# GLA on one core: ScalarE in written order, Exp and Ln from one table, a scratch in PSUM, token scales stored transposed, four weight casts on ScalarE

## The chip, the cores and the metric

One core of one Trainium2 chip. The metric is the device time of one execution in microseconds. The kernel before took 2317.13 us, the median of three runs (2316.85 to 2319.09).

## What is computed

One layer of a streaming encoder for 2048 prompt tokens and 32 sample tokens, model width 1024, all in float32. One projection feeds a windowed attention and a gated linear attention (GLA) side by side; their outputs are joined, projected and followed by a feed-forward part.

```python
n = rmsnorm(x);  z = n @ w_in                       # qa ka va | qg kg vg | rg | ca
log_a = log_sigmoid(ca @ w_alpha + b_alpha) / 16
# A: o = softmax(qa ka^T / 8, with a sink per head) va, over the own chunk of 64 and two before
# B, per chunk, with b = cumsum(log_a):
o_inter = (q * exp(b)) @ S
A = sum_k q[t] * exp(b[t] - b[s]) * k[s], s <= t;   o_intra = A @ v
S = exp(b_last) * S + (k * exp(b_last - b))^T @ v
gla = rmsnorm(o) * silu(rg)
h = x + concat(attn, gla) @ w_out
y = h + relu(rmsnorm(h) @ w_up)^2 @ w_down
```

## The kernel before

The prompt is cut into 16 tiles of 128 tokens; the sample is a seventeenth tile of 32. Every big product is made of three matmuls, since each operand is held as a rounded high part (`h`) and a remainder (`l`); `split_weight` (L194) loads a piece of a weight into a tile called `stage`, rounds it on ScalarE (L203) or VectorE (L205) and subtracts on GpSimd or VectorE (L207). `stage` and most other loads share five buffers, the io pool, so a load waits until a buffer comes free.

The work runs in three parts. In the **attention part** (0 to some 390 us) `front` (L253) loads a tile `xT1a` of transposed input, scales it and splits it into `nT`; `scales` computes the tile's rsqrt of the mean square into a column of `rstd`; `store` (L282) writes that column (`rs`) and the split tile (`nTh`, `nTl`) to DRAM, from where the GLA part reads them again. `project_q`, `project_kv` and `project_gate` make the projections, `attend` the softmax attention. Toward its end `prepare_gla` (L612) loads the GLA weights, each in two halves; `GLA_ENG` says for each half which engine rounds it and which subtracts.

In the **GLA part** (some 390 to 755 us) the tiles go in eight halves of two tiles (the first has the sample as a third). For each half `project` (L721) makes zq and zk, copied to `kq` with the token scales `rb` (rows of `rs` broadcast over the partitions, L631), and zv. `decay` (L641) makes the gates' logarithm for the next half: cc, then Abs, Exp and Ln on ScalarE, then a running sum (scan) on VectorE at L674; between Ln and the sum stands `gates` (L710), which loads `g` and applies Silu. `gla_tile` (L783) works on one tile: qkp, ec (Exp of the running sum), eight differences E on GpSimd, Abs and Exp of them on ScalarE in two groups of four, their products with k and q on VectorE (L823, L827); then the diagonal `dk` and its copy into `AT` (L839), the transposes of the last E into `dk` and their copy `kdT` (L854), the matmuls `A`, their masked copies into `AT` (L881 to L892), the output `go`, the state update `Sp` (L924), squares of the output `v<-go` (L930), `rsqrt` (L170, eleven small steps on VectorE), the gated output `g` (L936), its transposes and the copy `gT` (L945), stored to `mixT`. In the last half the first output weights `wo_00` to `wo_11` and mixed inputs `m0`, `m1` of the feed-forward part are loaded and split too (`prepare_ffn`, `load_mix`). The **feed-forward part** takes the rest.

TensorE's order is written by hand: every matmul depends on the one before it (`_pe`, L87), and generators that yield a number of nanoseconds are resumed by a clock (`tick`, L138). On ScalarE only the operations that need a function table are chained (`table`, L118); a table load is put in where the function asks for another one. Everything else on ScalarE, VectorE, GpSimd and in SP's queue of DMAs is ordered by a scheduler that simulates the engines.

Of the kernel before, what the change touches and what calls it, by code (L numbers as in the profile page):

```python
# [9 lines left out]
F32 = mybir.dt.float32  # L10
F32R = mybir.dt.float32r
I32 = mybir.dt.int32
AF = mybir.ActivationFunctionType
# [6 lines left out]
P = 128  # L20
# [7 lines left out]

class Builder:
    def __init__(self, ctx, tc, a, o, nt=NT, ffn=True):  # L30
# [3 lines left out]
        self.V, self.S, self.G, self.T, self.Q = nc.vector, nc.scalar, nc.gpsimd, nc.tensor, nc.sync  # L34
        pool = lambda name, bufs, **kw: ctx.enter_context(tc.tile_pool(name=name, bufs=bufs, **kw))
# [7 lines left out]
        tiles = list(range(nt)) + [nt]  # L43
# [5 lines left out]
        self.rsd = [dt([self.rows(t), 1], f"rs{t}") for t in tiles]  # L49
# [74 lines left out]

    def spawn(self, gen, delay=0):
        task = [self.clock + delay, self.seq, gen]
        self.seq += 1
        self.tasks.append(task)
        return task
# [40 lines left out]
    def rsqrt(self, ms, r, n, name, psum=False):  # L170

        V = self.V
        y = self.small.tile([P, 16], F32, tag="rsq_y", name=f"rsq_y_{name}")[:r, :n]
        if psum:
            q = self.ps_s(f"rsq_q_{name}")[:r, :n]
        else:
            q = self.small.tile([P, 16], F32, tag="rsq_q", name=f"rsq_q_{name}")[:r, :n]
# [53 lines left out]
    def attention_phase(self):  # L231
# [3 lines left out]
        with ExitStack() as ctx:  # L235
# [46 lines left out]
            def store(t):  # L282

                r = self.rows(t)
                Q.dma_start(self.rsd[t], self.rstd[:r, t : t + 1])
                if t == nt or t % 2:
                    for x, dst in zip(nT[t], self.nTd[t // 2]):
                        Q.dma_start(dst, x.bitcast(F32))

            order = [*range(10), nt, *range(10, nt)]  # L290
# [3 lines left out]
            V.memset(self.ones, 1.0)  # L294
            S.activation(self.rstd[:, :1], self.ones, AF.Square)
# [261 lines left out]
            for i, t in enumerate(order):  # L557
# [13 lines left out]
                if t == nt - 1:  # L571
                    self.prepare_gla(0)
# [21 lines left out]
    GLA_ENG = (("act", "pool"), ("dve", "dve"))  # L594
# [26 lines left out]
    def gla_tokens(self, h, tiles):  # L621
# [3 lines left out]
        off = 0  # L625
        for t in tiles:
# [4 lines left out]
            self.Q.dma_start(rb[:, off : off + r], self.rsd[t].rearrange("r o -> o r").broadcast_to([P, r]))  # L631
# [46 lines left out]
    def gla_phase(self):  # L678
        tc, a, V, S, G, Q = self.tc, self.a, self.V, self.S, self.G, self.Q
        nt = self.nt  # L680
        with ExitStack() as ctx:
# [28 lines left out]
            def gates(h):  # L710

                for t in halves[h]:
# [6 lines left out]
                    G.tensor_tensor(out=gv, in0=gv, in1=ggla[:r].unsqueeze(1).broadcast_to([r, 4, P]), op=ALU.mult)  # L719

# [62 lines left out]
            def gla_tile(n, t, off, kq, cc):  # L783
# [149 lines left out]
                rs = self.rsqrt(ss, L, 4, f"g{t}")  # L933
# [15 lines left out]
            gates(0)  # L949
            for h in range(len(halves)):  # L950
# [4 lines left out]
            self.finish()  # L955
            for key, name in (("p", "s_prompt"), ("s", "s_sample")):
# [488 lines left out]
```

## Time and profile before

| | |
|---|---|
| median of 3 runs | 2317.13 us (2316.85 to 2319.09) |
| profiled execution | 2316.26 us; its span 2314.5 us, mean TensorE clock 0.98 |
| TensorE busy | 2253.7 us (97%) |
| VectorE, ScalarE, GpSimd busy | 1410.0 us (61%), 953.1 (41%), 1197.4 (52%) |
| DMA | 221.56 MB, mean 96 GB/s |

The span is what the profile covers; the 1.8 us around it belong to the execution's own time. A row of a timeline begins with its start and duration in us; then come the engine, the line in the kernel, the operation and what it writes and reads; square brackets at the end give how long the engine had been idle before and what released it. In a row of windows stand the stretch, its length, for each of TensorE, its weight loads, VectorE, ScalarE and GpSimd the busy time with the number of instructions, then TensorE's granted clock as a share of full speed, the share of the DMA engines' time and GB/s. TensorE is called PE there, VectorE DVE, ScalarE ACT, GpSimd POOL; SPq is SP's queue of DMAs.

### The profile page before, as it was taken

What the parts mean: (1) busy time and instruction counts of PE and PEld (TensorE: products, weight loads), DVE (VectorE), ACT (ScalarE), POOL (GpSimd) and SP (SyncE); (2) the same over time, 40 slices, a digit from 0 to 9 for tenths busy, and PEclk for the clock granted to TensorE, in tenths of its full rate; (3) what the DMA queues carried; (4) which work ended last, traced back from release to release, by engine and by line L of the source; (5) the groups of instructions that cost most, each with busy time, mean ns of one, the idle gap of its engine ahead of it and who ended that gap; (6) DMA issues with size and microseconds to landing.
All of it is one profiled execution on the core that took longest, in us unless ns stands there. A gap on an engine that the chain in (4) does not pass through costs nothing.

```text
span 2314.5 us, 39745 instructions
## 1 busy us (share of the span) xinstructions
PE 2253.7 (97%) x15389; PEld 2117.4 (91%) x15389; DVE 1410.0 (61%) x3631; ACT 953.1 (41%) x1953; POOL 1197.4 (52%) x995
## 2 busy tenths in 40 slices
PE   7999999899998999999999999999999999999999
PEld 5777776788877999999999999999999999999999
DVE  7666657688887755555553755555554755555555
ACT  3554445455562643333334533333334533333331
POOL 3221224333241396667765566666665386666662
PEclk9999999889988999999999999999999999999999
DMA  8654563221322423222236222222227122222221
GB/s 233 140 107 107 145 173 125 84 73 66 106 82 81 128 78 97 82 74 74 73 109 185 74 73 74 73 73 73 74 63 219 55 74 73 73 74 73 74 64 52
DMA packets 154301, 221.56 MB, mean 96 GB/s; under 512 B 38224, under 2 KB 114976, under 8 KB 150272
## 3 DMA queue, kind: packets, MB, share of 16 engines
q1 hardware_dynamic: 154112, 219.02, 32.2%
q8 instruction: 121, 1.98, 0.4%
q14 instruction: 68, 0.56, 0.1%
HBM read 180.08 MB, written 38.91 MB: 95 GB/s over the span
## 4 chain that ended last, share of the span: by engine, by line
PE 74%; DVE 12%; DMA 5%; POOL 3%; issue 3%; ACT 2%; SPq 1%; POOLq 0%; DVEq 0%; ACTq 0%
PE dn L112 30%; PE PS4B L112 4%; PE PS3T L112 4%; PE PS2T L112 4%; PE PA22T L112 4%; PE PA11B L112 4%; PE PA12B L112 4%; PE PS1T L112 4%; PE zq L112 3%; PE op L112 3%; PE zr L112 3%; DVE AT L892 2%; PE zkv L112 2%; PE zv L112 2%; PE O L112 1%
## 5 line engine op out<-in xcount | busy, mean ns | idle before, releaser
L1103 POOL TENSOR_TENSOR wu<-stage,wu 128x512 fp32r<-128x512 f32 x336 | 432.5, 1299 | 468.3 <-ACT wu L1102 456.6
L1279 DVE TENSOR_TENSOR y<-y,dn 128x360 f32<-128x360 f32 (+1 forms) x768 | 393.0, 514 | 228.4 <-PE dn L112 225.5
L1102 ACT ACTIVATE wu<-stage 128x512 fp32r<-128x512 f32 x336 | 206.2, 628 | 493.6 <-PE dn L112 213.5
L1105 POOL TENSOR_TENSOR stage<-stage 128x512 f32<-128x512 f32 x192 | 249.4, 1299 | 7.5
L1232 ACT ACTIVATE r<-PA11B 128x360 f32<-128x360 f32 (+1 forms) x48 | 22.1, 460 | 284.4 <-PE PA11B L112 284.4
L1217 DVE TENSOR_TENSOR PA12B<-PA12B,r 128x360 f32<-128x360 f32 (+1 forms) x48 | 25.3, 526 | 150.2 <-PE PA12B L112 150.2
L719 POOL TENSOR_TENSOR g<-g,ggla 128x512 f32<-128x512 f32 (+1 forms) x17 | 25.0, 1489 | 170.4 <-ACT g L120 170.4
L112 PE MATMUL PA22T<-T4h,wu 128*128 128x360 f32 (+1 forms) x384 | 101.5, 328 | 0.0
L112 PE MATMUL PS3T<-T3h,wu 128*128 128x360 f32 (+1 forms) x384 | 100.1, 323 | 0.1
L112 PE MATMUL PS4B<-B22h,wu 128*128 128x360 f32 (+1 forms) x384 | 100.2, 324 | 0.0
L112 PE MATMUL PS1T<-T1h,wu 128*128 128x360 f32 (+1 forms) x384 | 98.9, 321 | 0.0
L112 PE MATMUL PA11B<-B11h,wu 128*128 128x360 f32 (+1 forms) x384 | 98.8, 321 | 0.0
L112 PE MATMUL PS2T<-T2h,wu 128*128 128x360 f32 (+1 forms) x384 | 98.7, 320 | 0.0
L112 PE MATMUL PA12B<-B21h,wu 128*128 128x360 f32 (+1 forms) x384 | 98.7, 321 | 0.0
L892 DVE COPY_PREDICATED AT<-masks,A 64x64 f32<-64x64 int32 (+1 forms) x330 | 82.9, 253 | 13.7 <-PE A L112 3.8
L816 POOL TENSOR_TENSOR E<-cc 128x256 f32<-128x256 f32 (+1 forms) x117 | 68.3, 622 | 25.3 <-PE A L112 19.5
L506 ACT ACTIVATE P<-S,negm 128x192 f32<-128x192 f32 (+2 forms) x128 | 51.6, 417 | 51.1 <-DVE negm L501 31.6
L112 PEld LDWEIGHTS PA22T<-T4h,wu 128*128 128x128 f32 x384 | 70.1, 193 | 0.0
L112 PEld LDWEIGHTS PS3T<-T3h,wu 128*128 128x128 f32 x384 | 69.1, 190 | 0.5 <-ACT T3h L1135 0.5
L112 PEld LDWEIGHTS PS4B<-B22h,wu 128*128 128x128 f32 x384 | 69.0, 190 | 0.0
L112 PEld LDWEIGHTS PS1T<-T1h,wu 128*128 128x128 f32 x384 | 68.1, 188 | 0.0
L112 PEld LDWEIGHTS PS2T<-T2h,wu 128*128 128x128 f32 x384 | 68.1, 188 | 0.0
(1008 smaller groups left out, 7736.5 us busy)
## 6 DMA issues: line engine op xcount, KB each, us to landing
stage<-in_w_up SPq DMA_DIRECT2D x96, 512.0 KB, 4.2
stage<-in_w_down SPq DMA_DIRECT2D x96, 512.0 KB, 3.9
stage<-in_w_out SPq DMA_DIRECT2D x24, 512.0 KB, 5.2
xT1a<-in_xT_prompt SPq DMA_DIRECT2D x16, 512.0 KB, 7.5
stage<-in_w_in SPq DMA_DIRECT2D x16, 512.0 KB, 5.3
x1a<-in_x_prompt SPq DMA_DIRECT2D x16, 512.0 KB, 6.9
out_yT_prompt<-y SPq DMA_DIRECT2D x32, 180.0 KB, 4.4
m<-mixT SPq DMA_DIRECT2D x11, 512.0 KB, 4.5
```

Of the source, the lines that this page charges most:

```text
L112: self._pe(self.T.matmul(out, lhsT, rhs, start=start, stop=stop), ns)
L506: S.activation(Pt[:, u, :n], sp[:, jp], AF.Exp, bias=negm[:, ch, u : u + 1], scale=0.125, accum_out=rsum[:, ch, u : u + 1],)
L719: G.tensor_tensor(out=gv, in0=gv, in1=ggla[:r].unsqueeze(1).broadcast_to([r, 4, P]), op=ALU.mult)
L816: G.tensor_tensor(out=e4, in0=c4, in1=ref, op=ALU.subtract)
L892: V.copy_predicated(dst, mk.unsqueeze(1).broadcast_to([L // nh, 2, w // m, m]), src[r].rearrange("s p (n m) -> s p n m", m=m),)
L1102: self.after(S.activation(h, src, AF.Copy), after)
L1103: G.tensor_tensor(out=l, in0=src, in1=f32(h), op=ALU.subtract)
L1105: tt = lambda o, x, y, op: G.tensor_tensor(out=o, in0=x, in1=y, op=op)
L1217: tt = lambda out, x, y, op=ALU.add: V.tensor_tensor(out=out, in0=x, in1=y, op=op)
L1232: S.activation(r0, product(b, "A11", "B11"), AF.Copy)
L1279: V.tensor_tensor(out=yg[:, f, :], in0=yg[:, f, :], in1=ps, op=ALU.add)
```

## The change

Five edits. ScalarE's handle is wrapped: while `on` is set, from the first gates to the end of the GLA part, every ScalarE instruction depends on the one before it, so that the engine runs them in the order in which the program writes them. `preload` asks for one function table that holds both Exp and Ln, at the start and after each `gates`; 17 table loads stand in the program in place of 25. The scratch `q` of the GLA rsqrt lies in unused columns of the tile `go` in PSUM. `rs` becomes one tensor of 17 rows by 128, written once, near the end of the attention part, from a transpose of `rstd`, and the `rb` loads read rows of it. `GLA_ENG` gives the rounding of the second half of each GLA weight piece to ScalarE (four casts of 128x1024).

```diff
@@ -26,12 +26,32 @@
 LEVELS = (64, 32, 16, 8, 4, 2, 1)
 
 
+class InOrder:
+
+
+    def __init__(self, eng, tc):
+        self.eng, self.tc, self.on, self.last = eng, tc, False, None
+
+    def __getattr__(self, name):
+        f = getattr(self.eng, name)
+
+        def call(*args, **kw):
+            ins = f(*args, **kw)
+            if self.on and self.last is not None:
+                self.tc.add_manual_dep(ins.ins, self.last.ins.name, NOSYNC, reason="order")
+            self.last = ins if self.on else None
+            return ins
+
+        return call
+
+
 class Builder:
     def __init__(self, ctx, tc, a, o, nt=NT, ffn=True):
         self.ctx, self.tc, self.nc, self.a, self.o = ctx, tc, tc.nc, a, o
         self.nt, self.with_ffn = nt, ffn
         nc = self.nc
         self.V, self.S, self.G, self.T, self.Q = nc.vector, nc.scalar, nc.gpsimd, nc.tensor, nc.sync
+        self.S = InOrder(self.S, tc)
         pool = lambda name, bufs, **kw: ctx.enter_context(tc.tile_pool(name=name, bufs=bufs, **kw))
         self.const = pool("const", 1)
         self.small = pool("small", 3)
@@ -46,7 +66,7 @@
 
         self.nTd = [[dt([P, KB, 2 * P if t < nt else NS], f"nT{x}{t}") for x in "hl"] for t in range(0, nt + 1, 2)]
         self.cad = [dt([16, self.rows(t)], f"ca{t}") for t in tiles]
-        self.rsd = [dt([self.rows(t), 1], f"rs{t}") for t in tiles]
+        self.rsd = dt([nt + 1, P], "rs")
         self.rgd = [dt([self.rows(t), 512], f"rgd{t}") for t in tiles]
 
         self.last_pe = self.last_table = None
@@ -122,6 +142,13 @@
             self.tc.add_manual_dep(ins.ins, self.last_table.ins.name, NOSYNC, reason="table order")
         self.last_table = ins
 
+    def preload(self):
+
+        ins = self.S.preload_act_table_set("natural_log_exp_and_others")
+        if self.last_table is not None:
+            self.tc.add_manual_dep(ins.ins, self.last_table.ins.name, NOSYNC, reason="table order")
+        self.last_table = ins
+
     def spawn(self, gen, delay=0):
         task = [self.clock + delay, self.seq, gen]
         self.seq += 1
@@ -167,13 +194,13 @@
         self.gemm(ps, xh, xl, lambda kb: w[kb // 4][0][:, kb % 4, :], lambda kb: w[kb // 4][1][:, kb % 4, :])
 
 
-    def rsqrt(self, ms, r, n, name, psum=False):
+    def rsqrt(self, ms, r, n, name, psum=False, q=None):
 
         V = self.V
         y = self.small.tile([P, 16], F32, tag="rsq_y", name=f"rsq_y_{name}")[:r, :n]
         if psum:
             q = self.ps_s(f"rsq_q_{name}")[:r, :n]
-        else:
+        elif q is None:
             q = self.small.tile([P, 16], F32, tag="rsq_q", name=f"rsq_q_{name}")[:r, :n]
         yi, qi = y.bitcast(I32), q.bitcast(I32)
         V.tensor_scalar(out=qi, in0=ms.bitcast(I32), scalar1=1, scalar2=None, op0=ALU.logical_shift_right)
@@ -281,17 +308,17 @@
 
             def store(t):
 
-                r = self.rows(t)
-                Q.dma_start(self.rsd[t], self.rstd[:r, t : t + 1])
                 if t == nt or t % 2:
                     for x, dst in zip(nT[t], self.nTd[t // 2]):
                         Q.dma_start(dst, x.bitcast(F32))
 
+            self.preload()
             order = [*range(10), nt, *range(10, nt)]
             eng = (("act", "pool"), ("dve", "dve"))
             gm = slice(self.g0, self.g0 + KB)
             Q.dma_start(self.packed[:, gm], a["packed"][:, gm])
             V.memset(self.ones, 1.0)
+            V.memset(self.rstd, 1.0)
             S.activation(self.rstd[:, :1], self.ones, AF.Square)
             front(order[0])
             wq = self.wide_pairs(w_in, 0, "wq", (("act", "dve", 2), ("act", "dve", 2)), (0,))
@@ -569,6 +596,12 @@
                 elif i > 1:
                     z[t] = project_kv(t, *project_q(t))
                 if t == nt - 1:
+
+                    pt = self.ps_s("rsT")[: nt + 1, :P]
+                    self.tr(pt, self.rstd)
+                    rsT = c.tile([nt + 1, P], F32, tag="rsT", name="rsT")
+                    S.activation(rsT, pt, AF.Copy)
+                    Q.dma_start(self.rsd, rsT)
                     self.prepare_gla(0)
                 self.spawn(attend_sample(*z.pop(t)) if t == nt else attend(t, *z.pop(t)))
                 if t != nt - 2:
@@ -591,7 +624,7 @@
             self.finish()
 
 
-    GLA_ENG = (("act", "pool"), ("dve", "dve"))
+    GLA_ENG = (("act", "pool"), ("act", "dve"))
 
     def load_gla_consts(self):
         a, c, Q, V = self.a, self.mid, self.Q, self.V
@@ -628,7 +661,7 @@
             if t == nt or t % 2 == 0:
                 for x, src in zip(pair, self.nTd[t // 2]):
                     self.Q.dma_start(x[:, :, off : off + src.shape[2]].bitcast(F32), src)
-            self.Q.dma_start(rb[:, off : off + r], self.rsd[t].rearrange("r o -> o r").broadcast_to([P, r]))
+            self.Q.dma_start(rb[:, off : off + r], self.rsd[t : t + 1, :r].broadcast_to([P, r]))
             off += r
         return pair, off, rb
 
@@ -717,6 +750,7 @@
                     self.table(g[:r], g[:r], AF.Silu)
                     gv = g[:r].rearrange("p (h v) -> p h v", h=4)
                     G.tensor_tensor(out=gv, in0=gv, in1=ggla[:r].unsqueeze(1).broadcast_to([r, 4, P]), op=ALU.mult)
+                self.preload()
 
             def project(h):
                 tiles = halves[h]
@@ -930,7 +964,7 @@
                     S.activation(sq[:L, hh * 256 : hh * 256 + 256].rearrange("t (p v) -> t p v", p=2), o[hh], AF.Square)
                 V.reduce_sum(ss, sq[:L].rearrange("t (h v) -> t h v", h=4), axis=AX.X)
                 V.tensor_scalar(out=ss, in0=ss, scalar1=1.0 / P, scalar2=EPS, op0=ALU.mult, op1=ALU.add)
-                rs = self.rsqrt(ss, L, 4, f"g{t}")
+                rs = self.rsqrt(ss, L, 4, f"g{t}", q=ps[0][:L, 256:260])
                 for hd in range(4):
                     cs = slice(hd * P, (hd + 1) * P)
                     V.scalar_tensor_tensor(
@@ -947,12 +981,14 @@
                 stage[n] = 4
 
             gates(0)
+            S.on = True
             for h in range(len(halves)):
                 if h + 1 < len(halves):
                     self.gla_toks[h + 1] = self.gla_tokens(h + 1, halves[h + 1])
                 project(h)
             self.prepare_ffn(3)
             self.finish()
+            S.on = False
             for key, name in (("p", "s_prompt"), ("s", "s_sample")):
                 for p in range(2):
                     for hh in range(2):
```

The order of instructions moves with it. SP's queue near its start, before: the loads of the scales `rb` and of constants stand ahead of `xT1a`, the load of tile 2 (names with numbers are tensors and buffers).

```order
L288 DMA nTl_93<-nT_0l 128x2048
L404 DMA ck<-in_cache_k 128x128
L405 DMA cv<-in_cache_v 128x128
L603 DMA wal<-in_w_alpha 16x256
L604 DMA d_2801<-in_resets 128x288
L605 DMA masks<-in_masks 128x224
L631 DMA rb_4265<-rs_127 128x128
L631 DMA rb_4265<-rs_128 128x128
L250 DMA xT1a_510<-in_xT_prompt 128x1024
```

The same place now:

```order
L343 DMA gk<-in_g_k 128x128
L313 DMA nTh_92<-nT_0h 128x2048
L313 DMA nTl_93<-nT_0l 128x2048
L431 DMA ck<-in_cache_k 128x128
L432 DMA cv<-in_cache_v 128x128
L636 DMA wal<-in_w_alpha 16x256
L637 DMA d_2775<-in_resets 128x288
L638 DMA masks<-in_masks 128x224
L277 DMA xT1a_494<-in_xT_prompt 128x1024
```

The two stores `rs` and the two loads `rb` are gone from here; eight places ahead of `xT1a` stood nTl and now stands gk.

VectorE at the end of the attention part, before: the casts of wqg and wkg among the rows of qk's rsqrt.

```order
L205 CAST wqgh<-stage 128x1024
L457 TENSOR_SCALAR qT_4011<-qTp_4000,packed 128x4x2x64
L396 COPY caT_4008<-kTp_4005 16x128
L207 TENSOR_TENSOR wqgl<-stage,wqgh 128x1024
L352 TENSOR_REDUCE ssqk_4032<-sq_3925 128x10
L350 TENSOR_SCALAR ca_4030<-zkv_3966,rstd 128x16
L205 CAST wkgh<-stage 128x1024
L353 TENSOR_SCALAR ssqk_4032<-ssqk_4032 128x10
L207 TENSOR_TENSOR wkgl<-stage,wkgh 128x1024
L179 TENSOR_SCALAR rsq_q_qk_4036<-ssqk_4032 128x10
```

The same rows now:

```order
L234 TENSOR_TENSOR wqgl<-stage,wqgh 128x1024
L379 TENSOR_REDUCE ssqk_4001<-sq_3894 128x10
L377 TENSOR_SCALAR ca_3999<-zkv_3935,rstd 128x16
L380 TENSOR_SCALAR ssqk_4001<-ssqk_4001 128x10
L206 TENSOR_SCALAR rsq_q_qk_4005<-ssqk_4001 128x10
L207 TENSOR_SCALAR rsq_y_qk_4004<-rsq_q_qk_4005 128x10
```

The two casts have gone to ScalarE, and the subtraction wkgl stands further down, among the steps of rsqrt.

ScalarE in one half of the GLA part, before: from the load of Silu's table over the second tile's kdT to E of the first tile of this half and the squares `v<-go`.

```order
L120 ACT_TABLE_LOAD
L120 ACTIVATE g_6417<-g_6417 128x512
L120 ACTIVATE g_6429<-g_6429 128x512
L120 ACT_TABLE_LOAD
L120 ACTIVATE ec_6665<-cc_6408 128x256
L854 ACTIVATE kdT_6490<-dk_6436 128x256
L818 ACTIVATE E_0_6669<-E_0_6669 128x1024
L120 ACTIVATE E_0_6669<-E_0_6669 128x1024
L818 ACTIVATE E_1_6680<-E_1_6680 128x1024
L120 ACTIVATE E_1_6680<-E_1_6680 128x1024
L818 ACTIVATE E_0_6762<-E_0_6762 128x1024
L945 ACTIVATE gT_6583<-gTp_6578 128x512
```

One half later in the changed kernel (all of ScalarE's rows bear L39, the line of the wrapper):

```order
L39 ACT_TABLE_LOAD
L39 ACTIVATE g_6904<-g_6904 128x512
L39 ACTIVATE gT_6913<-gTp_6908 128x512
L39 ACTIVATE g_6916<-g_6916 128x512
L39 ACT_TABLE_LOAD
L39 ACTIVATE kdT_6978<-dk_6924 128x256
L39 ACTIVATE gT_7065<-gTp_7060 128x512
L39 ACTIVATE v_6724<-go_8_7080 128x256
L39 ACTIVATE v_6724<-go_8_7081 128x256
L39 ACTIVATE ec_7152<-cc_6895 128x256
L39 ACTIVATE E_0_7156<-E_0_7156 128x1024 x2
L39 ACTIVATE E_1_7167<-E_1_7167 128x1024 x2
```

kdT has moved ahead of ec; ec and E of the next tile now stand behind gT and the squares of an earlier tile.

## Rows read from the trace of the kernel before

**Rows 1.** The page, part 1: busy us, share of the span, instructions.

```profile
PE 2253.7 (97%) x15389; PEld 2117.4 (91%) x15389; DVE 1410.0 (61%) x3631; ACT 953.1 (41%) x1953; POOL 1197.4 (52%) x995
```

**Rows 2.** Windows: stretch, length, busy us of five engines, TensorE's clock, DMA share, GB/s.

```profile
100.00:320.00 220.00, 220.00 (x1261) 169.39 (x1261) 139.48 (x541) 107.19 (x345) 52.34 (x90) 1.00 0.51 121
...
390.00:500.00 110.00, 102.14 (x1006) 83.86 (x1005) 79.33 (x276) 57.27 (x84) 38.55 (x57) 0.88 0.21 69
500.00:660.00 160.00, 154.79 (x1780) 132.36 (x1778) 138.09 (x492) 84.09 (x123) 49.80 (x72) 0.96 0.26 90
660.00:760.00 100.00, 88.49 (x895) 78.69 (x888) 72.63 (x230) 38.83 (x61) 28.41 (x24) 0.86 0.32 92
760.00:2310.00 1550.00, 1543.03 (x9670) 1539.42 (x9669) 861.74 (x1748) 585.89 (x1120) 972.12 (x679) 1.00 0.28 85
```

**Rows 3.** TensorE's waits, 320 to 780: us in total, times, the longest.

```profile
PE go L112 <- ACT kdT L854: 6.0, 3, 3.1
PE dk L116 <- DVE rsq_y_g L180: 5.1, 4, 3.1
...
PE dk L116 <- DVE AT L839: 4.0, 2, 3.2
```

**Rows 4.** Timeline of TensorE: start, us, instruction, [idle before <-releaser].

```profile
49.10 0.49 PE L112 MATMUL zq<-wq0h,nT_2h 128*128 128x512 f32 x1 [2.35 <-ACT nT_2h L271]
...
359.17 1.09 PE L116 MATMUL qTp<-packed,qk 128*128 128x128 f32 x4 [4.63 <-DVE es L383]
...
430.74 0.66 PE L116 MATMUL dk<-packed,E 128*128 128x128 f32 x2 [3.21 <-DVE AT L839]
...
659.18 0.44 PE L116 MATMUL dk<-packed,E 128*128 128x128 f32 x2 [0.66 <-DVE rsq_y_g L180]
...
679.62 0.65 PE L112 MATMUL go<-Sp,Qc 64*128 64x128 f32 x2 [3.10 <-ACT kdT L854]
...
707.62 0.69 PE L116 MATMUL dk<-packed,E 128*128 128x128 f32 x2 [3.15 <-DVE rsq_y_g L180]
```

**Rows 5.** Timeline of SP's queue, 28.9 to 46 us.

```profile
30.38 0.43 SPq L288 DMA_DIRECT2D nTl<-nT_0l  x1
...
43.95 0.33 SPq L250 DMA_DIRECT2D xT1a<-in_xT_prompt  x1
```

**Rows 6.** DMA issues, 28 to 46 us: KB each, median us to landing.

```profile
nTl<-nT_0l SPq DMA_DIRECT2D x1, 1024.0 KB, 13.5
```

**Rows 7.** Timeline of VectorE, end of the attention.

```profile
345.84 2.54 DVE L205 CAST wqgh<-stage 128x1024 fp32r<-128x1024 f32 x1 [8.04 <-DMA stage<-in_w_in]
...
351.16 2.30 DVE L205 CAST wkgh<-stage 128x1024 fp32r<-128x1024 f32 x1
...
358.20 0.83 DVE L356 TENSOR_TENSOR qk<-qk,rsq_y_qk 128x640 f32<-128x640 f32 x1
```

**Rows 8.** Timeline of ScalarE, the same stretch.

```profile
344.26 1.06 ACT L203 ACTIVATE wqgh<-stage 128x1024 fp32r<-128x1024 f32 x1 [5.25 <-DMA stage<-in_w_in]
```

**Rows 9.** Timeline of ScalarE, one half of the GLA part.

```profile
511.65 1.28 ACT L120 ACT_TABLE_LOAD   x1
...
517.77 0.42 ACT L120 ACTIVATE ec<-cc 128x256 f32<-128x256 f32 x1 [2.38 <-DVE cc L674]
```

**Rows 10.** Timeline of VectorE, the half from 618 to 657 us.

```profile
643.36 0.61 DVE L924 SCALAR_TENSOR_TENSOR Sp<-Sp,ec,go 128x128 f32<-128x128 f32 x2
...
649.39 0.41 DVE L827 TENSOR_TENSOR E<-E,kq 128x256 f32<-128x256 f32 x1
```

**Rows 11.** Groups by form on VectorE: GLA part, then the feed-forward part.

```profile
L183 DVE SCALAR_TENSOR_TENSOR rsq_q_g<-rsq_q_g,ssg 128x4 f32<-128x4 f32 x48 | 7.7, 161 | 1.3
...
L183 DVE SCALAR_TENSOR_TENSOR rsq_q_y<-rsq_q_y,msy 80x8 f32<-80x8 f32 x3 | 0.5, 170 | 0.1
```

**Rows 12.** Timeline of ScalarE, the half from 618 to 657 us.

```profile
638.02 1.06 ACT L818 ACTIVATE E<-E 128x1024 f32<-128x1024 f32 x1 [2.02 <-POOL E L816]
...
656.08 0.38 ACT L930 ACTIVATE v<-go 128x256 f32<-128x256 f32 x1 [7.06 <-DVE rsq_q_g L182]
```

## The prediction

> **What bounds the kernel now.** I began with the page's busy times: TensorE is busy for 97% of the span [rows 1], so a step elsewhere counts only where TensorE waits for it or where its clock is held down. The windows show where that is [rows 2]. From 760 us to the end, in the feed-forward part that the change leaves alone, TensorE is busy for 1543.03 of 1550 us at clock 1.00: nothing to win there. In the GLA part it is idle for 7.9 us from 390 to 500, for 5.2 from 500 to 660 and for 11.5 from 660 to 760, 24.6 in all. The granted clock costs more on top: (1 - 0.88) x 110 = 13 us, (1 - 0.96) x 160 = 6 us, (1 - 0.86) x 100 = 14 us, together 33. So this part has at most some 58 us to give back, and the attention ahead of it single waits.
>
> The waits name the releasers [rows 3]: kdT on ScalarE three times, rsqrt rows and the copy L839 on VectorE. The timeline gives single waits, the first number in the brackets being TensorE's idle time [rows 4]: 4.63 us at 359.17 (the end of the attention), 3.21 at 430.74, 3.10 at 679.62, 3.15 at 707.62.
>
> **The change, part by part.** I price each part by the wait of TensorE that it touches.
>
> *Token scales, SP's queue at the start.* In the program each of SP's DMAs waits for the one eight places ahead of it on the queue. Before, the load of tile 2 (xT1a at 43.95) stands eight behind the store nTl, issued at 30.38 [rows 5], which took 13.5 us to land [rows 6]: 43.88. TensorE then waits 2.35 us for that tile [rows 4]. Without the two rs stores and two rb loads ahead of it, the load stands eight behind g_k, which is issued before the stores, and can go out some 8 us sooner. It then shares the DMA engines with nTh and nTl, so I don't count 8 us, only most of the wait: **-2**, between 0 (it still lands with the stores) and -5. The other fifteen small stores take room on SP's queue but lie beside 100 to 320 us, where TensorE is busy for 220.00 of 220 [rows 2]; the added transpose, copy and store are one instruction on each of three engines, too small to count.
>
> *Four rounding casts from VectorE to ScalarE, at the end of the attention.* Two of them stand on VectorE ahead of qk, for which TensorE waits 4.63 us: 2.54 + 2.30 = 4.84 us [rows 7]. On ScalarE the same cast takes 1.06 us, and that engine had sat idle for 5.25 us before it, waiting for the same load [rows 8]. VectorE's end of qk would fall from 359.03 to 354.2, when TensorE runs dry (359.17 - 4.63 = 354.54). But some rows between take maxima of scores that TensorE makes in those same microseconds and can't come sooner, so I leave a quarter of the wait, 1.2 us: **-3.4**, between 0 and the whole -4.63. The Trainium skill, "ScalarE: Activation LUTs", Rules for kernel authors, speaks against this move: cheap elementwise work belongs on VectorE, which is faster per element. By that rule the term would be 0 or a small loss. The rows here show the cast at 2.54 and 2.30 us on VectorE and at 1.06 us on ScalarE, so in this place the trace decides for the move.
>
> *ScalarE in written order, kdT ahead of ec.* Before, kdT stands behind ec, and ec waits 2.38 us for a scan on VectorE [rows 9]; the three waits for kdT sum to 6.0 us, the longest 3.1 [rows 3], there with two w_out casts ahead as well. Now kdT follows the second table load, behind no scan. I let all three go, the two shorter ones at 1.45 us each.
>
> *One table for Exp and Ln.* Each half's chain loses one load of 1.28 us [rows 9]; eight in all, 10.2 us of an engine that is 41% busy [rows 1]. Behind it come Ln and VectorE's scan, which now wait less; I count that inside the next step only.
>
> *VectorE's rows behind that.* The eight E products of a half's second tile, 0.41 us each [rows 10], move behind L839, so that L839, for which TensorE waits 4.0 us in two places [rows 3], comes up to 3.3 us earlier.
>
> *The rsqrt scratch in PSUM.* The same instructions: 161 ns with the scratch in SBUF in this part, 170 with it in PSUM in the later one [rows 11]. Some 170 instructions by 10 ns are 2 us of VectorE at most, partly exposed: 0, ends +2 and -1.
>
> By stage:
> - 390 to 500: L839 from 3.21 to about 1, -2.2, and one kdT wait, -1.45: **-3.7**. Ends 0 and -14 (half of the 7.9 us idle and most of the 13 us of clock).
> - 500 to 660: one kdT wait, -1.45; the three short waits for rsqrt rows (5.1 less the 3.15 of the last half), -2; and of the 6 us of clock what follows the kdT wait, about -2.5: **-6**. Ends 0 and -11, all that is lost there. VectorE, busy for 138.09 of 160 us [rows 2], is the next limit.
> - 660 to 760: kdT -3.1, half of the 3.15 at 707.62 -1.6; against it +1.7, for E of tile 14 now stands on ScalarE behind four casts of w_out weights, whose loads wait for free slots, and kdT of tile 14 behind two more: **-3**. Ends +8 and -10.
>
> Sum: 2 + 3.4 + 3.7 + 6 + 3 = 18.1. The profiled execution took 2316.26 us, 0.87 below the median of 2317.13. 2316.26 - 18.1 = 2298.2, on the median's scale **2299**.
>
> **The rivals.**
>
> *Half of it.* The next thing is right behind each wait that goes: VectorE, at 86% from 500 to 660, becomes the limit, no clock comes back, the tail gives nothing. -2 -2 -2 -2 = -8: **2309**. For it: VectorE's rows are already named in most waits [rows 3]. Against: the kdT waits are ScalarE's own.
>
> *The clock comes back.* Beyond the 2.5 us already counted, half of the 33 us of held-down clock goes with the waits: 18.1 + 14 = 32, **2285**. The stages with the long waits are those with the low clock [rows 2]; but some waits remain in each.
>
> *Slower: the squares hold back E.* In written order the squares of an earlier tile (v<-go) stand ahead of ec and E of the next tile on ScalarE, and everything behind waits with them. Before, E of the half shown began at 638.02, and one of the squares came at 656.08 after 7.06 us of waiting for VectorE [rows 12]. The point that decides: TensorE needs that tile's products at 659.18 [rows 4]; eight of them take some 3 us, four E operations of 1.06 us 4.2 and ec 0.4, so the squares must end by about 651.5. They wait for the state update, which VectorE did at 643.36 [rows 10]; E would then end near 649, just as VectorE reached its products at 649.39. If the squares come so late that one group of E (4.2 us) is exposed in each of six halves, that is +25 on the forecast: **2324**. In the last half the w_out casts can do the same once, +8, which alone doesn't turn the sign.
>
> *Nothing changes.* ScalarE is 41% busy, what leaves it or comes to it was covered, and each wait freed is met by another: **2317**.
>
> **How the numbers follow.** A measurement of this kernel can tell about 0.2%, 4.6 us, from no change. Chances: forecast 0.50 (its own range 2290 to 2307), half of it 0.20, the clock 0.11, nothing 0.08, squares 0.11. The range 2281 to 2319 takes in all but the squares' case and a little of the clock's. Faster by over 0.2%: 0.50 + 0.11 + most of 0.20 = 0.80; within 0.2%: 0.09; slower: 0.11.
>
> **What would show it.** Right: the tile-2 load issued on SP before 40 us, and no wait over 1 us near 49; the wait for qk at the end of the attention under 2 us; kdT gone from TensorE's waits; 17 table loads; 500 to 660 shorter by about 6 us. Wrong: E on ScalarE idle for go or the state update, and TensorE waiting behind it; kdT of tile 14 waiting for a w_out load; or VectorE busy for over 95% with TensorE waiting for its rows as before.

## The result, and the profile after

The changed kernel takes 2290.31 us (median of 4 runs, 2286.99 to 2292.86) beside 2317.32 us for the kernel before on the same chip: ratio 0.9881, 95% interval 0.9864 to 0.9898, so 27 us faster. Measured a second time it came to 2288.69 against 2322.30, ratio 0.9853 (0.9839 to 0.9866), some 34 us. The forecast was 2299 in a range of 2281 to 2319. The sign and the range held; the gain was half as large again as the sum of 18.1 us (nearly twice by the second measurement). Two of its steps rested on a wrong mechanism: the one at the start, and the one in the GLA part, where TensorE's waits hardly shrank in sum; there the size came out in part by luck.

The profiled execution took 2291.81 us, span 2290.0. To compare stages I cut the spans at the same matmuls of TensorE: the first zq of tile 4, zr of tile 14, zq of the second, fourth and eighth half, the first product with m1. In the profile after, these fall at 87.78, 336.20, 398.59, 487.24, 633.70 and 730.02 us. Its windows, cut there (columns as in [rows 2]); a half is a pair of tiles, and "halves 2 and 3" is the stage from 398.59 us, "halves 4 to 7" the one from 487.24:

```profile
0.00:87.78 87.78, 75.77 (x396) 60.85 (x397) 68.94 (x222) 42.88 (x119) 31.35 (x44) 0.96 0.60 202
87.78:336.20 248.42, 248.42 (x1437) 191.73 (x1436) 155.87 (x598) 123.67 (x388) 61.35 (x100) 1.00 0.39 138
336.20:398.59 62.39, 60.25 (x370) 44.71 (x367) 37.86 (x98) 34.10 (x83) 25.97 (x37) 0.97 0.36 120
398.59:487.24 88.65, 81.19 (x877) 69.56 (x876) 72.34 (x260) 43.67 (x64) 26.47 (x40) 0.87 0.20 69
487.24:633.70 146.46, 145.69 (x1729) 125.31 (x1728) 129.74 (x474) 79.32 (x116) 47.32 (x72) 0.98 0.28 98
633.70:730.02 96.32, 81.88 (x910) 73.33 (x908) 71.34 (x231) 38.67 (x60) 26.26 (x24) 0.91 0.31 93
730.02:2290.00 1559.98, 1547.10 (x9682) 1542.76 (x9680) 863.37 (x1749) 586.58 (x1121) 971.56 (x679) 0.99 0.28 85
```

Before, the same stages took 94.66, 248.44, 67.21, 92.11, 154.51, 101.56 and 1556.01 us. The gain lies in five of them. In the first and the third it is idle time of TensorE that went (17.7 to 12.0 us in the first, 7.5 to 2.1 in the third). The three stages of the GLA part are another matter. Before they read:

```profile
410.31:502.42 92.11, 84.25 (x877) 71.40 (x876) 71.82 (x256) 45.47 (x65) 27.07 (x40) 0.85 0.19 67
502.42:656.93 154.51, 149.95 (x1729) 128.32 (x1728) 132.80 (x466) 82.94 (x120) 49.80 (x72) 0.96 0.26 90
656.93:758.49 101.56, 89.39 (x910) 79.22 (x908) 75.50 (x243) 39.55 (x62) 28.41 (x24) 0.87 0.32 94
```

TensorE's idle time went from 7.9 to 7.5 us in halves 2 and 3, from 4.6 to 0.8 in halves 4 to 7, and in the last half it grew, from 12.2 to 14.4. So of the 16.8 us that these stages gained only 1.9 are waits; the other 14.8 are busy time, for the same number of matmuls. The granted clock rose in all three stages (0.85 to 0.87, 0.96 to 0.98, 0.87 to 0.91); by (1 - clock) x length it cost some 33 us before and 23 after, so it gave back about 10. By the second profiles of both kernels it is 3.9 us of waits and 15.1 of busy time. What the remaining 3 to 5 us of busy time are stays open.

TensorE's waits up to 780 us (answers to [rows 3]: us in total, times, longest):

```profile
PE zq L132 <- ACT wq0h L39: 6.5, 1, 6.5
PE dk L136 <- DVE E L857: 5.6, 1, 5.6
PE gTp L136 <- DVE g L970: 4.9, 1, 4.9
PE A L132 <- ACT gT L39: 4.1, 1, 4.1
PE zkv L132 <- DVE rsq_y_a L211: 3.2, 1, 3.2
PE go L132 <- DVE g L970: 2.2, 1, 2.2
```

kdT no longer holds a go (it holds an A for 1.0 us and a dk for 0.6), and the 4.63 us for qk and the 2.35 us for tile 2 [rows 4] are gone. Three waits are new: 4.1 us for gT at 452 us, 5.6 for E and 4.9 for g in the last half.

The load of tile 2 on SP's queue (answers to [rows 5]), 10 us sooner, of which 3.4 are that the store nTl itself goes out sooner:

```profile
26.96 0.43 SPq L313 DMA_DIRECT2D nTl<-nT_0l  x1
...
33.99 0.33 SPq L277 DMA_DIRECT2D xT1a<-in_xT_prompt  x1
```

ScalarE in a half: kdT right behind the second table load (answers to [rows 9]); and two halves later, E behind the squares, which the slower rival feared (answers to [rows 12]):

```profile
452.70 1.28 ACT L39 ACT_TABLE_LOAD   x1
453.99 0.38 ACT L39 ACTIVATE kdT<-dk 128x256 f32<-128x256 f32 x1
...
554.48 0.39 ACT L39 ACTIVATE v<-go 128x256 f32<-128x256 f32 x1 [2.50 <-DVE rsq_y_g L211]
...
556.76 4.19 ACT L39 ACTIVATE E<-E 128x1024 f32<-128x1024 f32 x4
```

The square waits 2.50 us for VectorE with E behind it, and TensorE does not wait for that E: the next dk that waits at all, at 573.20, waits 0.78 us for the copy of the diagonal (L839 before, L873 now).

### The profile page after: what moved, and what is told of

Its sections match the earlier page's. It is cut to its first block, busy times and chain, and to the rows that moved or that the text cites. A ratio compares the mean times of both kernels' runs of the same rounds, so it can differ in the third digit from the quotient of the medians.

```text
span 2290.0 us, 39728 instructions
## 1 busy us (share of the span) xinstructions
PE 2240.3 (98%) x15390; PEld 2108.2 (92%) x15390; DVE 1399.5 (61%) x3628; ACT 948.9 (41%) x1950; POOL 1190.3 (52%) x995
## 4 chain that ended last, share of the span: by engine, by line
PE 84%; DVE 7%; DMA 2%; ACT 2%; issue 2%; POOL 2%; SPq 0%; POOLq 0%; ACTq 0%; DVEq 0%
PE dn L132 30%; PE zq L132 5%; PE PS4B L132 4%; PE zv L132 4%; PE zr L132 4%; PE PS3T L132 4%; PE PA22T L132 4%; PE PS2T L132 4%; PE PA11B L132 4%; PE PA12B L132 4%; PE PS1T L132 4%; PE op L132 3%; PE zkv L132 2%; DMA stage<-in_w_out 2%; PE zk L132 2%
## 5 line engine op out<-in xcount | busy, mean ns | idle before, releaser
L39 ACT ACTIVATE wu<-stage 128x512 fp32r<-128x512 f32 x336 | 206.3, 628 | 490.2 <-PE dn L132 215.1
L39 ACT ACTIVATE r<-PA11B 128x360 f32<-128x360 f32 (+1 forms) x48 | 22.1, 460 | 286.1 <-PE PA11B L132 286.0
L39 ACT ACTIVATE P<-S,negm 128x192 f32<-128x192 f32 (+2 forms) x128 | 51.6, 417 | 47.2 <-DVE negm L528 28.9
L546 POOL TENSOR_TENSOR P<-P,es 128x512 f32<-128x512 f32 x15 | 15.6, 1041 | 102.2 <-ACT sq L39 43.0
```

Of the source, the lines that this page charges most:

```text
L39: ins = f(*args, **kw)
L546: (G if ch == 0 else V).tensor_tensor(out=dst, in0=src, in1=rb, op=ALU.mult)
```

## The experiments

Four kernels (u1 to u4) each undo one edit, two (b) make one edit alone, two (c, e) alter the written order, three (d, g and before again) measure something by itself. They ran on three chips: u1 to u4 on one, the change again, b and c on another, d to g on a third. The first table gives the time against the kernel before on the same chip (its median was 2317.3 us beside the change, then 2326.8, 2322.3 and 2321.7, so ratios are compared, not times); the second gives each stage of the profiled execution less that of the first profile of before, in us. There is no profile of before from the chip of u1 to u4, where its median was 9.5 us longer, so their columns are safest compared with one another.

| kernel | median us | ratio (95% interval) |
|---|---|---|
| change; again | 2290.31; 2288.69 | 0.9881 (0.9864 to 0.9898); 0.9853 (0.9839 to 0.9866) |
| u1, no written order | 2297.62 | 0.9877 (0.9863 to 0.9891) |
| u2, 25 table loads | 2296.24 | 0.9869 (0.9856 to 0.9883) |
| u3, small rs stores | 2302.28 | 0.9894 (0.9879 to 0.9909) |
| u4, casts on VectorE | 2290.86 | 0.9853 (0.9833 to 0.9873) |
| b, rs alone | 2309.88 | 0.9944 (0.9932 to 0.9956) |
| b, written order alone | 2311.88 | 0.9953 (0.9940 to 0.9965) |
| c, tail order | 2291.99 | 0.9866 (0.9851 to 0.9881) |
| d, tiny DMAs | 2290.49 | 0.9865 (0.9844 to 0.9886) |
| e, free gT and w_out | 2286.57 | 0.9846 (0.9831 to 0.9861) |
| g, scratch in SBUF | 2290.84 | 0.9865 (0.9850 to 0.9880) |

| stage | change; again | u1 | u2 | u3 | u4 | rs alone | order alone | c | d | e | g | before again |
|---|---|---|---|---|---|---|---|---|---|---|---|---|
| start, to zq of tile 4 | -6.9; -7.6 | -6.2 | -6.4 | +1.9 | -7.7 | -6.3 | +1.9 | -7.2 | -7.2 | -6.2 | -5.6 | +1.1 |
| end of attention | -4.8; -6.4 | -6.4 | -6.4 | +0.1 | -2.8 | -3.2 | +1.4 | -4.8 | -6.3 | -6.4 | -6.4 | +1.5 |
| halves 2 and 3 | -3.5; -3.5 | -0.9 | -1.8 | -2.7 | -2.2 | +3.3 | -1.6 | -3.5 | -2.8 | -3.5 | -2.1 | +1.6 |
| halves 4 to 7 | -8.1; -10.1 | -3.1 | -6.9 | -8.1 | -7.7 | -1.9 | -7.9 | -8.0 | -10.0 | -10.0 | -10.1 | -1.7 |
| last half | -5.2; -5.5 | -5.4 | -3.1 | -3.2 | -5.9 | -0.5 | -2.9 | -3.4 | -1.4 | -8.0 | -4.4 | 0.0 |
| feed-forward | +4.0; +4.6 | +6.4 | +5.8 | -0.6 | +2.6 | +5.7 | +5.4 | +2.6 | +5.2 | +3.6 | +3.1 | +1.0 |

The stage from zq of tile 4 to zr of tile 14 is left out of it (within 0.5 us everywhere). A stage repeats within some 2 us between profiles of one kernel, so smaller entries say nothing.

### One edit undone at a time

```diff
# u1: the scheduler orders ScalarE again
-            S.on = True
# u2: 25 table loads again
-            self.preload()
...
-                self.preload()
# u3: a store of 128 separate elements per tile again, rb loads back at the queue's start
+                Q.dma_start(self.rsd[t], self.rstd[:r, t : t + 1])
...
# u4: the four casts on VectorE again
-    GLA_ENG = (("act", "pool"), ("act", "dve"))
+    GLA_ENG = (("act", "pool"), ("dve", "dve"))
```

> Everything of the change except ScalarE's written order, which is left to the scheduler again. Theory (the written order, by putting kdT ahead of ec and E, is what the GLA part gained): the stretch from the first zq of the second half of tiles to the first matmul with m1 comes back by most of the 16.8 us that it lost (354.5 to 320 us or so being the other parts), so 2300 to 2306 us, with kdT again among TensorE's waits; the start and the end of the attention keep their gain. Rival (the table load taken out of each half did it, and the order is beside the point): under 4 us slower than the changed kernel.

> Everything of the change except the one table for Exp and Ln: 25 table loads again, written order kept. Theory: the eight loads of 1.28 us lie beside other work except at the start of the GLA part: 0 to +4 us on the changed kernel. Rival (the table loads are what the GLA part gained): +8 to +15 us.

> Everything of the change except the transposed token scales: seventeen small stores and the two loads rb at the start of SP's queue again. Theory (the tile-2 load was held behind the store nTl): the wait for tile 2 near 49 us comes back, and with it the later one near 78 us and the lost clock behind it: +5 to +7 us on the changed kernel, all of it before 100 us. Rival (the start's 6.9 us come from the table preload or another order of VectorE): within 1.5 us of the changed kernel.

> Everything of the change except that the four casts of 128x1024 are back on VectorE. Theory: the wait for qk at the end of the attention comes back, +3 to +5 us, all of it between the last zkv and the first zq of the GLA part. Rival (VectorE is not what qk waits for; the weights landed sooner because SP's queue is shorter): under 1.5 us.

**u1.** The halves 2 to 7 lose 7.6 of the 11.5 us that the change gained there (9.6 of 13.6 by its second profile), and kdT is back among TensorE's waits from 330 to 765 us:

```profile
PE go L132 <- ACT kdT L39: 4.9, 3, 3.6
PE dk L136 <- DVE rsq_y_g L207: 4.0, 3, 3.2
```

Against u3 and u4, profiled on the same chip, the loss in these halves is 5.9 to 6.8 us. So the order is worth some 6 to 10 us there, at most somewhat over half of the 16.8 that were to come back, and nothing in the last half, where it was expected to gain too. kdT is only a part of it: of its 4.9 us the longest, 3.6, lies in the last half, and 0.6 in each of the two stages that lost; halves 2 and 3 also wait 2.8 us for ec. By time u1 takes 6.8 us more than u4, but its ratio, 0.9877, lies between the change's two, so the timed runs alone don't show the loss; the time of the order alone, below, does show a gain.

**u2.** Expected 0 to +4; the stages from 398 us to the first m1 product lose 4.9 us against the change's first profile and 7.2 against its second, and the ratio lies between the change's two. Against u3 and u4 the same stages lose 2.2 and 3.9. So the loads lie at most a little more on the path than the theory had it, and less than the rival.

**u3.** The start loses 8.8 us, more than the 5 to 7 expected, and against the expectation the loss does not end there: the end of the attention loses all of its gain, although the casts are on ScalarE. There, ScalarE stands still for a weight load and the copy that TensorE needs stands behind the cast. Timeline of ScalarE in u3, then of TensorE:

```profile
349.21 1.06 ACT L39 ACTIVATE wqgh<-stage 128x1024 fp32r<-128x1024 f32 x1 [7.81 <-DMA stage<-in_w_in]
350.18 0.85 ACT L39 ACTIVATE pS<-pT 128x512 f32<-128x512 f32 x2
```

```profile
350.81 1.01 PE L132 MATMUL O<-pS,v 128*64 128x256 f32 x4 [4.46 <-ACT pS L39]
```

**u4.** The end of the attention loses 2.0 us (3.6 against the second profile), a little under what was expected; over the whole run the ratio is that of the change. And the casts are short on VectorE now (groups by form, VectorE, 320 to 400 us of u4: busy us, mean ns of one, idle before):

```profile
L232 DVE CAST wqgh<-stage 128x1024 fp32r<-128x1024 f32 x1 | 0.7, 694 | 2.1 <-DMA stage<-in_w_in 2.1
...
L232 DVE CAST wkgh<-stage 128x1024 fp32r<-128x1024 f32 x1 | 0.7, 670 | 0.0
```

So 2.54 and 2.30 us [rows 7] are not what VectorE needs for this cast. At those moments GpSimd was subtracting another weight piece (timeline of GpSimd in before, the first of the two):

```profile
345.45 2.37 POOL L207 TENSOR_TENSOR wqgl<-stage,wqgh 128x1024 fp32r<-128x1024 f32 x1 [11.83 <-ACT wqgh L203]
```

The subtraction ends at 347.82, the cast that began in it at 348.38. The fourteen profiles hold 104 such casts on VectorE. The 49 that began while a subtraction of 128x1024 ran on GpSimd each ended 0.55 to 0.62 us after that subtraction; the other 55 took 0.67 to 0.70 us. With the loads landed early, the two casts of u4 above began with no subtraction running.

### One edit alone

> The changed kernel itself once more, beside the others of this call and with a second profile, to see how far its stages repeat. Both theories: its ratio to the kernel before between 0.986 and 0.990; each stage up to 760 us within 1 us of the first profile, the feed-forward part within 4.

> The kernel before with the transposed token scales alone. Theory (after the run that undid them): they take away the waits near 49 and 78 us and let the GLA weights land sooner at the end of the attention, so -7 to -9 us before 100 us and -2 to -5 us between the last zr of the even tile 14 and the second half's zq; -9 to -14 us in all. Rival (they only work together with the other edits, above all with the casts on ScalarE): -5 to -8 us in all, none of it after 100 us.

> The kernel before with ScalarE's written order in the GLA part alone, 25 table loads kept. Theory (order is worth what the run without it lost): from the second half's zq to the last half's zq -6 to -10 us, no kdT among TensorE's waits there; the last half unchanged to +3; nothing before 390 us: -5 to -9 us in all. Rival (the order pays only with the shorter table chain): within 3 us of the kernel before.

The change again: its ratio, 0.9853, lies just below the expected 0.986 to 0.990; its stages repeat within 1 us but for two, which came out 1.5 and 2.0 us shorter (both with less lost clock). The kernel before with the new `rs` alone gains 12.4 us in 2322.3 (ratio 0.9944; 0.0056 x 2322 = 13.0): 6.3 at the start (7 to 9 were expected), 3.2 at the end of the attention. Its theory held in the sum and in the second place, and its rival, nothing after 100 us, did not; the stages of its profile add up to only -2.9, since halves 2 and 3 and the feed-forward part came out longer there. With the written order alone it gains 0.0047 x 2322 = 10.9, in halves 2 to 7 and, unexpectedly, 2.9 in the last half. Both intervals lie clear of 1. The two together make some 24 of the 27 to 34 us.

### What the small stores cost

```diff
# d: on top of the change, SP's queue at its old length
+                Q.dma_start(self.dum[t], self.rstd[:1, t : t + 1])     # one element, at the place of each rs store
...
+            for i in range(2):
+                Q.dma_start(row[:, i : i + 1], a["g_k"][:1, i : i + 1])  # one element, where rb stood
```

> The changed kernel with seventeen DMAs of a single 4-byte element at the old places of the rs stores and two loads of one element where rb stood, so that SP's queue has its old length and every DMA stands eight places behind the same one as before; only the 128 elements per store are missing (what they write and read is used nowhere). Theory as predicted (the tile-2 load is late because it stands eight behind nTl): the start is slow again, +5 to +9 us before 100 us. Rival (the 128 separate elements of each store hold up the DMA engines, and with them nTl and the weight loads behind): the start and the end of the attention stay as fast as in the changed kernel, within 2 us, and the loads after the store of tile 14's scales land in under 10 us in place of 16.

The rival holds. At the start every DMA stands eight behind the same one as in the kernel before, and the start is still as fast (-7.2); xT1a goes out at 35.93, not at 43.95 [rows 5] (timeline of SP's queue in d):

```profile
29.00 0.43 SPq L315 DMA_DIRECT2D nTl<-nT_0l  x1
...
35.93 0.35 SPq L278 DMA_DIRECT2D xT1a<-in_xT_prompt  x1
```

The load does wait for nTl, as the prediction had it, in before and, much less, in d (waits of SP's queue from 20 to 60 us):

```profile
SPq L250 <- DMA nTl<-nT_0l: 3.5, 1, 3.5
```

```profile
SPq L278 <- DMA nTl<-nT_0l: 0.7, 1, 0.7
```

What differs is nTl, which took 13.5 us to land in before [rows 6] and takes 7.3 in the change. So it was not the queue's length but the store of separate elements. d leaves out the bytes of the two rb loads as well, but these went out only from 37.93 us on, when the DMA had been slow for some 6 us already (a window of before; last columns: TensorE's clock, DMA share, GB/s; d has 278 GB/s there):

```profile
32.00:38.00 6.00, 6.00 (x40) 5.46 (x39) 5.61 (x24) 1.77 (x6) 3.24 (x9) 1.00 0.70 27
```

The end of the attention is as fast as in the change, too (-6.3). d's profile gives no landing times, so the sign of under 10 us can't be read, and it was set too low: the change itself has 9.2 to 12.7 us there. The four casts of these weights begin at 331.26 to 338.26 in d and at 331.98 to 338.99 in the change; in before the first begins at 344.26 [rows 8].

The DMA queue's rows of before, of the change and of d (packets, MB, share of 16 engines' span):

```profile
q1 hardware_dynamic: 154112, 219.02, 32.2%
```

```profile
q1 hardware_dynamic: 151778, 219.02, 29.8%
```

```profile
q1 hardware_dynamic: 151816, 219.02, 29.8%
```

The same megabytes, 2334 packets fewer, and the engines' time falls from 0.322 x 2314.5 x 16 = 11924 us to 0.298 x 2290.0 x 16 = 10919: 1005 us. The time is not in the small packets themselves: by the trace's records a packet of 4 bytes takes 0.01 us on average in either kernel (11185 of them before, 8834 in the change). It is in the large ones beside them. Before, 224 packets, 206 of them of 4096 or 8192 bytes, took over 2 us each, 842 us in all, each within 15 us behind the issue of a store. In the four profiles with the stores 224 to 284 packets did, in the ten without them 0 to 3 (in d 2). The mean packet of 4096 bytes fell from 0.24 to 0.20 us, the longest from 8.6 to 2.5. Why large packets stand still beside such a store, no run shows. The DMA issues of before from 326 to 346 us, and the same four loads in the change, 319 to 336 us (KB, median us to landing):

```profile
stage<-in_w_in SPq DMA_DIRECT2D x4, 512.0 KB, 16.3
...
rs<-rstd SPq DMA_DIRECT2D x1, 0.5 KB, 14.9
```

```profile
stage<-in_w_in SPq DMA_DIRECT2D x4, 512.0 KB, 11.3
```

And a window of before in which the engines' time is taken and little moves (56 GB/s; the mean is 96):

```profile
335.00:340.00 5.00, 5.00 (x35) 4.44 (x36) 2.59 (x9) 2.14 (x4) 0.00 (x0) 1.00 1.25 56
```

The Trainium skill, "DMA: Bandwidth & Descriptors", Rules for kernel authors, says that a last dimension without contiguous elements lowers to one descriptor per element and should be rearranged. The trace's counts agree: the seventeen stores have 16 x 128 + 32 = 2080 elements, and 2334 packets went with them.

### The last half, and the order made freer

```diff
# c: loads and casts of m0 and the first w_out weights behind E of tile 14, in the program's text
-                if h == len(halves) - 1:
-                    self.prepare_ffn(1)
-                    self.prepare_ffn(0)
...
+                    if h == len(halves) - 1 and i == 0:
+                        self.prepare_ffn(1)
+                        self.prepare_ffn(0)
...
# e: an operation issued while `free` is set neither waits for the last one nor is waited for
+            if self.free:
+                return ins
...
+        self.S.free = True      # around prepare_ffn, and around the copy gT
```

> The changed kernel with the program text of the last half altered: the loads and casts of m0 and of the first w_out weights are written behind the E operations of tile 14 in place of ahead of them. Theory (E of tile 14 waits in line behind four casts whose weights have not landed, and TensorE waits 5.6 us for it): that wait falls under 2 us and the last half is 3 to 6 us shorter than in the changed kernel. Rival (the wait only changes its name, since the w_out products then come late): within 1.5 us, with a new wait of some 4 us on op<-m0h.

> The changed kernel with the copies gT and ScalarE's operations for the feed-forward part (m0, m1, w_out casts and the copies of their products) left out of the written order. Theory (the three long waits that are left, 4.1 us for gT near 452 and 5.6 and 4.9 in the last half, come from the order's head of line): the first goes, the last half is 2 to 6 us shorter, 4 to 9 us in all. Rival (they come from VectorE's rows and late weights): under 2 us gained, the waits under other names.

In the change, E of tile 14 did stand in line behind the casts, as the prediction had it (timeline of ScalarE, then the matmul that waits):

```profile
662.90 1.06 ACT L39 ACTIVATE wo_00h<-stage 128x1024 fp32r<-128x1024 f32 x1 [3.33 <-DMA stage<-in_w_out]
666.09 1.06 ACT L39 ACTIVATE wo_00h<-stage 128x1024 fp32r<-128x1024 f32 x1 [2.12 <-DMA stage<-in_w_out]
...
669.97 4.17 ACT L39 ACTIVATE E<-E 128x1024 f32<-128x1024 f32 x4
```

```profile
677.34 0.66 PE L136 MATMUL dk<-packed,E 128*128 128x128 f32 x2 [5.59 <-DVE E L857]
```

**c** takes that wait away and gains nothing: the last half is 1.9 us longer. The waits of c from 630 to 740 us show one long wait for g in place of the two of 5.6 and 4.9 us, and not on the op that I had named:

```profile
PE gTp L136 <- DVE g L970: 11.5, 1, 11.5
PE op L132 <- DVE AT L926: 2.9, 1, 2.9
```

**e** shortens the last half by 2.7 us (2.5 against the second profile). The wait for gT goes too, but halves 2 and 3 take as long as before it; from 398 to 490 us another wait has its place:

```profile
PE dk L134 <- DVE g L972: 3.8, 1, 3.8
```

Its ratio, 0.9846, is the lowest measured; its interval lies just below the first of the change's (0.9861 against 0.9864) but overlaps the second, so it is not shown to be faster.

### Before again, and the scratch in SBUF

> The kernel before once more, for a second profile. If the 4 us by which the feed-forward part was longer in the profiles of the changed kernel are chance (which matmuls the low clock falls on), the stretch from the first m1 product to the end takes 1559 to 1562 us here too, in place of 1556.0; if the change costs them, 1555 to 1557 again. The stages before it repeat within 2 us.

> The changed kernel with the rsqrt scratch of the GLA part back in SBUF. Both ends of the prediction: the stages within 2 us of the changed kernel; if the small steps are slower or faster with PSUM, their mean differs by more than 20 ns.

The second profile of before has 1557.0 us in the feed-forward part, the first 1556.0; eleven of the twelve other profiles have 1558.6 to 1562.4, u3 has 1555.5. Waits stand at the same three places in this part of each profile (near 770, 1270 and 1820 us in the change's); between before and the change they differ by some 2 us in sum, and so does the clock lost behind them. Chance alone is doubtful with so many on one side, yet no single edit accounts for it, since order alone and rs alone both show it; it stays open. The scratch in SBUF or PSUM makes no difference that shows: the three rsqrt steps take 170, 160 and 181 ns in SBUF and 171, 167 and 159 in PSUM. The last differs by more than the 20 ns of the expectation, but before, in SBUF too, it took 160.

## Why the prediction was right, and where it was not

**Start, -2: undersized, and for a wrong reason.** The load did stand eight behind nTl and wait for it; the step that failed is to price that place in the queue and to take nTl's 13.5 us as its own. Measured -6.9 and -7.6; in d the load stands there still and the gain is the same, and d and u3 put it down to the stores' single elements, which hold up nTl and the weight loads. Besides the wait for tile 2 [rows 4], a wait of 1.85 us at 77.79 went, which I had not counted; the stage's mean clock is 0.96 in both kernels. The part about the fifteen other stores lying beside other work was wrong at one place: the store of tile 14's scales, with the weight loads behind it.

**End of the attention, -3.4: the size nearly right (-4.8, -6.4), the cause half right.** The casts off VectorE are worth 2 to 3.6 us, but only where the weights land soon: rs alone gives 3.2, the casts without it 0.1. I took 2.54 and 2.30 us as VectorE's price; with the loads early it is 0.69 and 0.67, below ScalarE's 1.06. So the rule of the Trainium skill that the prediction named ("ScalarE: Activation LUTs", Rules for kernel authors), that VectorE is faster per element for cheap work, agrees with these rows, and [rows 7] showed a disturbed case. The disturbance goes with the subtractions on GpSimd: each cast that began in one ended right behind it, in every profile. No run moved the subtractions by themselves.

**390 to 500, -3.7: the size right, by luck.** Measured -3.5. The waits for L839 and kdT went about as forecast (3.2 to 0.3, 1.5 to 0.6), but 4.1 us for gT came in their place: idle time fell by only 0.4 us where the sum had 3.65, and the rest is busy time, some 2 us of it the clock.

**500 to 660, -6: right in mechanism.** Measured -8.1 (-10.1). Idle time fell by 3.8 us, where the sum had 3.45, and the clock gave back some 3, where it had 2.5. The kdT waits went with the written order, and a part of them came back in u1. The table loads, which I had only counted within the next step, are worth 1 to 5 us of this stage and the one before it, by u2 against u3, u4 and the change. VectorE, busy for 129.74 of 146.46 us, did not become the limit.

**Last half, -3: -5.2, but not by its waits.** The waits for kdT and the rsqrt rows went (3.3 to 1.0 and 3.8 to none, where the sum had -3.1 and -1.6), and a wait of 4.5 us for the state update, which the sum had left out, shrank to 1.2. Yet idle time grew by 2.3 us: the +1.7 for E behind the w_out casts was too small, and a wait of 4.9 us for g was new. The gain is 7.5 us of busy time, some 4.5 of it the clock, which this stage's sum had not counted. The casts ahead of E cost a wait of 5.6 us, and kdT of tile 14 came behind the last w_out cast, for whose weights ScalarE waited 4.07 us; TensorE waited 0.96 us for that kdT. Moving the first casts did not win the price back (c).

**Rsqrt scratch, 0: right.** **Feed-forward, 0:** +4.0 in the profile, open.

**The rivals.** The squares did stand ahead of E and did wait, 2.50 us at 554, but E was still in time: the squares end 8.2 us ahead of that tile's first dk, at 563.09, where the deciding point was some 7.6, so there was little to spare. The rival of the clock had the larger part of the GLA part right: some 10 of its 33 us came back (12 by the second profiles), fewer than its 16.5 but far more than the 2.5 of the sum, and that made up for the waits that stayed.

## What to carry to other kernels

A store of one column is small in bytes and large in packets: look at the DMA's share beside its GB/s, and at what lands behind such a store, before calling it hidden. Price an operation from a row only after asking what else ran in that row's time; another schedule may have a quite different duration for it. When a stage gets shorter, compare idle and busy time between the same two matmuls before crediting the waits that went: here the clock gave back more than they did. And where two edits meet in one wait, undo each alone and make each alone: here the casts were worth nothing or 2 to 3.6 us, depending on the stores.

## What was not expected of the hardware

Seventeen stores of single 4-byte elements, whose own packets take 0.01 us each, went with some 1000 us more of DMA engine time in packets of other transfers. 0.5 KB so written took 14.9 us to land, and the four weight loads behind it 15.7 to 16.5 us in place of 9.2 to 12.7. A cast on VectorE that began during a subtraction on GpSimd ended 0.55 to 0.62 us behind it, 49 times of 49. Small VectorE steps can meet this too: in the changed kernel one step of qk's rsqrt on 128x10 elements takes 2.24 us instead of 0.17 (timeline of VectorE) and ends at 341.54, just behind a subtraction that ends at 341.51 (timeline of GpSimd):

```profile
339.30 2.24 DVE L209 TENSOR_TENSOR rsq_q_qk<-rsq_y_qk 128x10 f32<-128x10 f32 x1
```

```profile
339.10 2.41 POOL L234 TENSOR_TENSOR wkgl<-stage,wkgh 128x1024 fp32r<-128x1024 f32 x1
```
